# The gated one-hot of a PEER router: one VectorE instruction per token in place of a compare and a ScalarE product

## The chip, the cores and the metric

The kernel runs on one core of a Trainium2 chip. The metric is the device time of one execution in microseconds, given as the median of several runs. Engines are named as in the profile: PE is TensorE (PEld its weight loads), DVE is VectorE, ACT is ScalarE, POOL is GpSimd, and SP issues DMAs.

## What is computed

Two layers, each a mixer with four branches followed by a PEER product-key expert layer, on 512 positions of width 1024. The change lies in the PEER part:

```
sc = einsum("thpd,pkd->thpk", q, sub_keys)            # 8 heads, 2 x 128 keys
s_top, i_top = top_k(sc, 16)
best, pos = top_k(all 16 x 16 sums of s_top, 16)
idx  = i_top0[pos // 16] * 128 + i_top1[pos % 16]      # expert number: first key * 128 + second key
gate = softmax(best)
act  = gelu(expert_u[idx] . h) * gate
out  = sum over the chosen experts of act * expert_v[idx]
```

There are 16384 experts, and each position chooses 128 of them (8 heads with 16 each), every choice with its gate.

## The kernel before

For the first three tiles of 128 positions (ND = 3) the experts are computed densely: `up` multiplies every block of 128 experts with the 384 positions, and the result is later multiplied by a gate matrix that is zero for experts that were not chosen. The fourth tile is computed by gathering expert rows (`gathered`), one row of each position at a time.

All bulk matrix products go through `Stream`: `load` brings 512 KB of weights by an SP DMA, `split` makes two parts of them, `wh` by an ACT cast (L108) and `wl` by a DVE subtraction (L109), and the PE does three products (L120, L122, L123). One call of `bulk` is called a **bulk** below: in the stretch in question it has 24 matmuls of 384 columns, eight on L120 and eight each on L122 and L123. `advance` splits the weights two bulks ahead (SA = 2); there are three `wh` buffers and two `wl` buffers. After a bulk, `up` evicts the result by an ACT activation (L1278) and stores it.

Work that isn't bulk runs beside it: generators are put into `Beside`, and before every bulk `tick` takes as many of their pieces as a rate allows. So the order of instructions on each engine is fixed in the program: pieces of the generators, the bulk's matmuls, the split for two bulks later, the eviction. Each engine takes its instructions strictly in that order.

`Router.dense` builds the gate matrix at rate RG = 3.1. For each of the three tiles it first runs `pairs` (candidates, top 16, softmax: a long run of DVE instructions), then transposes the first key, the second key and the gate into `RT`, and then does 32 **steps** of four positions each. A step compares a row of numbers 0..127 (`iota`) with the keys of each position, which gives for each position two one-hot matrices of 128 choices by 128 keys (`oh`, DVE, L1229). The one of the first key is multiplied by the gates (ACT, L1232, four instructions, each in place). Five steps later (LAG = 5) the PE multiplies the two for each of the four positions (L1218), and ACT copies the sum into the gate matrix `GB` (L1220). A step costs 1.3 of the rate, so two or three steps fall to one bulk. At the end of a tile the last five steps have no one-hot of their own and come together. Six such runs of 32 steps exist, three in each layer. Beside them runs `gathered` at rate 0.8: a POOL gather (L1250) and a DVE product with a sum (L1259) for one row.

Of the kernel before, what the change touches and what calls it, by code (L numbers as in the profile page):

```python
# [13 lines left out]
AF = mybir.ActivationFunctionType  # L14
OP = mybir.AluOpType
# [51 lines left out]
def bc(ap, shape):  # L67
    return ap.to_broadcast(shape)
# [256 lines left out]
def small(e, name, shape):  # L325
    return e.ps.tile(list(shape), F32, name=name, tag="s")
# [770 lines left out]
class Router:  # L1097
# [89 lines left out]
    def dense(self, gbp, GB0):  # L1187

        e, pb, l = self.e, self.pb, self.l
        nc = e.nc  # L1190
        V = nc.vector
        stores = []
        iota = pb.tile([128, 128], F32, name="iota128", bufs=1)
        nc.gpsimd.iota(iota, pattern=[[1, 128]], base=0, channel_multiplier=0, allow_small_or_imprecise_dtypes=True)

        def store(i, n):
            if i % n == 1 and stores:
                stores.pop(0)()
        for t in range(ND):
            R = pb.tile([128, 4, 128], F32, name="R")  # L1200
            for i, cost in enumerate(self.pairs(t, R)):
                store(i, 4)
                yield cost
            yield 3.5
            pt = small(e, "rT", [128, 3, 128])
            for i in range(3):
                nc.tensor.transpose(pt[:, i], R[:, i], e.ident)
            RT = pb.tile([128, 3, 128], F32, name="RT", bufs=1)
            nc.scalar.copy(RT, pt)
            yield  # L1210
            GB = gbp.tile([128, 2, 128, 64], F32, name="GB", tag="GB")
            ohs = {}
            for q in range(32 + LAG):
                if q >= LAG:
                    pg = small(e, "G", [128, 4, 128])
                    oh = ohs.pop(q - LAG)
                    for a in range(4):
                        nc.tensor.matmul(pg[:, a], oh[:, 1, a], oh[:, 0, a], start=True, stop=True)  # L1218
                    h, o = divmod((q - LAG) * 4, 64)
                    nc.scalar.copy(GB[:, h, :, o:o + 4], pg.rearrange("p a i -> p i a"))  # L1220
                    if o == 60 and t < ND - 1:
                        for i in range(0, 128, 32):
                            stores.append(lambda i=i, t=t, h=h, GB=GB: nc.scalar.dma_start(
                                e.dG[l][t, h][:, i:i + 32], GB[:, h, i:i + 32]))
                store(q, 3)
                if q < 32:

                    oh = ohs[q] = pb.tile([128, 2, 4, 128], F32, name="oh", tag="oh", bufs=OH)
                    V.tensor_tensor(out=oh, in0=bc(iota[:, None, None, :], [128, 2, 4, 128]),  # L1229
                                    in1=bc(RT[:, 0:2, q * 4:q * 4 + 4, None], [128, 2, 4, 128]), op=OP.is_equal)  # L1230
                    for a in range(4):
                        nc.scalar.activation(oh[:, 0, a], oh[:, 0, a], AF.Copy, scale=RT[:, 2, q * 4 + a:q * 4 + a + 1])  # L1232
                yield 1.3 if q < 32 else 0.2
        for f in stores:
            f()
        e.GB = GB
# [128 lines left out]
def peer(e, l, src, dst, out):  # L1365
# [4 lines left out]
    with ExitStack() as st:  # L1370
# [5 lines left out]
        with pool("rt") as p1, pool("rtb", 2) as pb, pool("ga", 2) as ga:  # L1376
            SC = gbp.tile([128, 16, NT, 128], F32, name="SC", tag="GB")
            r = Router(e, l, p1, pb, SC)
            sc = r.scores()
            for hp in range(16):  # L1380
                r.query(hp)
                if hp == 0:
                    B.add(sc, 1.0, 1)
            b = 0
            for b in range(2):
                up(e, l, b, ga)
            B.finish(sc)
            R = pb.tile([128, 4, 128], F32, name="R")
            first = B.add(r.pairs(NT - 1, R), RF)
            for b in range(2, 2 + NB1):  # L1390
                up(e, l, b, ga)
            B.finish(first)
            if l:
                V.tensor_scalar(R[:, 3], R[:, 3], float(l * 16384), None, op0=OP.add)
            V.tensor_copy(e.gidx, R[:, 3])
            V.tensor_copy(e.ggate, R[:, 2])
            dense = B.add(r.dense(gbp, None), RG)
            rows = B.add(gathered(e, l), RU)
            for b in range(2 + NB1, NS):
                up(e, l, b, ga)  # L1400
            B.finish(dense)
# [177 lines left out]
```

## Time and profile before

| what | us |
|---|---|
| median of 3 runs | 4107.23 |
| lowest and highest run | 4102.68 and 4108.01 |
| the profiled execution | 4096.73 |
| its span, first to last instruction | 4095.0 |
| PE busy | 3905.9 (95%) |
| DVE busy | 3105.0 (76%) |
| ACT busy | 1688.7 (41%) |
| POOL busy | 1625.0 (40%) |
| L1229, the compare, 192 times | 225.0 (1219 ns each) |
| L1232, the product, 768 times | 244.4 (392 ns each) |

Busy time is the time in which an engine has an instruction of its own running; records of the PE overlap, so a busy PE isn't a PE at its peak. The chain that ended last names the PE for most of what it could follow, so a stage is read by asking what the PE does there and what it waits for. The mean granted clock of the PE was 0.982 of full speed.

### The profile page before, as it was taken

How to read it: one execution, taken by the hardware profiler on the slowest of the kernel's cores; microseconds unless marked ns; L12 is line 12 of the kernel's file. 1: busy time of each engine (PE TensorE's matmuls, PEld its weight loads, DVE VectorE, ACT ScalarE, POOL GpSimd, SP SyncE). 2: the span in 40 equal slices, each digit the busy share in tenths (PEclk: the TensorE clock that was granted, in tenths of full speed). 3: DMA queues.
4: the chain of work that ended last, by engine and by line, in shares of the span. 5: the costliest groups of instructions: out<-in, count | busy, mean ns of one | idle time of the engine just before them, and what ended most of it. 6: DMA issues, size and time to landing. Idle time of an engine off the chain costs nothing. (4 is left out here: it accounts for less than half of the span.)

```text
span 4095.0 us, 56429 instructions
## 1 busy us (share of the span) xinstructions
PE 3905.9 (95%) x19994; PEld 3384.6 (83%) x19994; DVE 3105.0 (76%) x5101; ACT 1688.7 (41%) x2939; POOL 1625.0 (40%) x1566
## 2 busy tenths in 40 slices
PE   7899999999999999999989999999999999999998
PEld 5777777899998899888767777878999898998876
DVE  5667844898878677889867777448978877788997
ACT  4323233336575533333343233333365664333333
POOL 3410500022313467888653014000323225678995
PEclk9999999999999999999999999999999999999999
DMA  3323333346876799999923233342568768999997
GB/s 112 102 81 101 101 96 109 115 162 204 293 235 221 254 325 319 351 356 339 325 69 105 91 95 101 98 134 85 182 213 274 249 207 285 323 321 349 335 340 262
DMA packets 346651, 851.40 MB, mean 208 GB/s; under 512 B 43648, under 2 KB 164864, under 8 KB 342016
## 3 DMA queue, kind: packets, MB, share of 16 engines
q1 hardware_dynamic: 236048, 492.39, 36.1%
q0 software_dynamic: 74016, 272.66, 19.5%
q10 hardware_dynamic: 36304, 82.74, 5.5%
q8 instruction: 158, 2.59, 0.3%
q14 instruction: 125, 1.02, 0.1%
HBM read 754.60 MB, written 93.06 MB: 207 GB/s over the span
## 5 line engine op out<-in xcount | busy, mean ns | idle before, releaser
L109 DVE TENSOR_TENSOR wl<-wr,wh 128x1024 fp32r<-128x1024 f32 (+2 forms) x792 | 987.3, 1247 | 528.7 <-ACT wh L108 453.8
L122 PE MATMUL mm<-hh,wh 128*128 128x384 f32 (+1 forms) x3456 | 1240.8, 359 | 0.0
L123 PE MATMUL mm<-hl,wh 128*128 128x384 f32 (+1 forms) x3456 | 1239.9, 359 | 0.0
L108 ACT CAST wh<-wr 128x1024 fp32r<-128x1024 f32 (+2 forms) x792 | 787.8, 996 | 338.9 <-PE va L132 127.8
L120 PE MATMUL mm<-hh,wl 128*128 128x384 f32 (+1 forms) x3456 | 792.2, 371 | 68.6 <-DVE wl L109 64.0
L120 PEld LDWEIGHTS mm<-hh,wl 128*128 128x128 f32 x3456 | 623.1, 191 | 150.7 <-DVE wl L109 81.3
L122 PEld LDWEIGHTS mm<-hh,wh 128*128 128x128 f32 x3456 | 655.8, 190 | 56.9
L123 PEld LDWEIGHTS mm<-hl,wh 128*128 128x128 f32 x3456 | 654.9, 190 | 56.1
L1250 POOL DMA_INDIRECT row<-in_u_dram,gidx x256 | 345.3, 1349 | 721.9 <-DVE row L1259 664.0
L132 PE MATMUL va<-wh,al 128*128 128x512 f32 x1536 | 598.1, 389 | 1.3 <-DVE al L109 1.3
L131 PE MATMUL va<-wh,ah 128*128 128x512 f32 x1536 | 597.9, 389 | 0.0
L1169 POOL TENSOR_TENSOR eq<-eq,cidx 128x800 f32<-128x800 f32 x64 | 126.2, 1977 | 891.4 <-DVE eq L1167 885.7
L1250 POOL DMA_INDIRECT row<-in_v_dram,gidx x256 | 383.2, 1497 | 103.8 <-DVE gacc L1270 47.0
L1270 DVE SCALAR_TENSOR_TENSOR gacc<-row,z,gacc 128x1024 f32<-128x1024 f32 x254 | 394.6, 1553 | 11.8 <-DMA row<-in_v_dram,gidx 10.1
L129 PE MATMUL va<-wl,ah 128*128 128x512 f32 x1536 | 395.0, 391 | 4.8 <-DVE wl L109 3.3
L1259 DVE SCALAR_TENSOR_TENSOR row<-row,h2row 128x1024 f32<-128x1024 f32 x256 | 339.3, 1335 | 1.2 <-DMA row<-in_u_dram,gidx 1.1
L132 PEld LDWEIGHTS va<-wh,al 128*128 128x128 f32 x1536 | 288.3, 188 | 62.7 <-DVE al L109 1.7
L129 PEld LDWEIGHTS va<-wl,ah 128*128 128x128 f32 x1536 | 285.4, 188 | 66.1 <-issue 11.0
L131 PEld LDWEIGHTS va<-wh,ah 128*128 128x128 f32 x1536 | 288.3, 188 | 60.7
L108 ACT CAST ah<-as 128x384 fp32r<-128x384 f32 x256 | 130.9, 511 | 480.7 <-POOL as L1321 266.9
L109 DVE TENSOR_TENSOR al<-as,ah 128x384 fp32r<-128x384 f32 x256 | 172.5, 674 | 193.6 <-ACT ah L108 185.5
L1232 ACT ACTIVATE oh<-oh,RT 128x128 f32<-128x128 f32 x768 | 244.4, 392 | 100.4 <-DVE oh L1229 100.4
(345 smaller groups left out, 4472.6 us busy)
## 6 DMA issues: line engine op xcount, KB each, us to landing
wr<-in_uT_dram SPq DMA_DIRECT2D x256, 512.0 KB
wr<-in_v_dram SPq DMA_DIRECT2D x256, 512.0 KB
wr<-in_w_in_dram SPq DMA_DIRECT2D x144, 512.0 KB
dS<-act ACTq DMA_DIRECT2D x184, 192.0 KB
as<-dS SPq DMA_DIRECT2D x184, 192.0 KB
dG<-GB ACTq DMA_DIRECT2D x32, 1024.0 KB
ag<-dG SPq DMA_DIRECT2D x128, 256.0 KB
wr<-in_w_query_dram SPq DMA_DIRECT2D x32, 512.0 KB
```

The costliest lines, as they stand in the source:

```text
L108: e.nc.scalar.copy(hi, src)
L109: e.nc.vector.tensor_tensor(out=lo, in0=src, in1=hi, op=OP.subtract)
L120: e.nc.tensor.matmul(ps, al, bh, start=start and i == 0, stop=False)
L122: e.nc.tensor.matmul(ps, ah, bh, start=False, stop=False)
L123: e.nc.tensor.matmul(ps, ah, bl, start=False, stop=stop and i == n - 1)
L129: e.nc.tensor.matmul(ps, ah, bl, start=start, stop=False)
L131: e.nc.tensor.matmul(ps, ah, bh, start=False, stop=False)
L132: e.nc.tensor.matmul(ps, al, bh, start=False, stop=stop)
L1232: nc.scalar.activation(oh[:, 0, a], oh[:, 0, a], AF.Copy, scale=RT[:, 2, q * 4 + a:q * 4 + a + 1])
L1250: nc.gpsimd.indirect_dma_start(out=g, out_offset=None, in_=e.I["u" if n < 128 else "v"], in_offset=bass.IndirectOffsetOnAxis(ap=e.gidx[:, ...
L1259: V.scalar_tensor_tensor(g, g, 1.0, e.h2row, op0=OP.mult, op1=OP.mult, accum_out=z[:, k:k + 1])
L1270: V.scalar_tensor_tensor(e.gacc, g, z[:, k:k + 1], e.gacc, op0=OP.mult, op1=OP.add)
```

## The change

The compare on L1229 now makes only the one-hot of the second key (512 elements per partition where there were 1024). The one-hot of the first key and its product with the gate become one DVE instruction for each position: `iota` is compared with the key and the result is multiplied by the gate, and both are read as one value per partition from `RT`. The four ACT instructions of a step are gone. Nothing else differs; lines below L1232 move down by one.

```
                     oh = ohs[q] = pb.tile([128, 2, 4, 128], F32, name="oh", tag="oh", bufs=OH)
-                    V.tensor_tensor(out=oh, in0=bc(iota[:, None, None, :], [128, 2, 4, 128]),
-                                    in1=bc(RT[:, 0:2, q * 4:q * 4 + 4, None], [128, 2, 4, 128]), op=OP.is_equal)
+                    V.tensor_tensor(out=oh[:, 1], in0=bc(iota[:, None, :], [128, 4, 128]),
+                                    in1=bc(RT[:, 1, q * 4:q * 4 + 4, None], [128, 4, 128]), op=OP.is_equal)
                     for a in range(4):
-                        nc.scalar.activation(oh[:, 0, a], oh[:, 0, a], AF.Copy, scale=RT[:, 2, q * 4 + a:q * 4 + a + 1])
+                        t_ = slice(q * 4 + a, q * 4 + a + 1)
+                        V.tensor_scalar(oh[:, 0, a], iota, RT[:, 0, t_], RT[:, 2, t_], op0=OP.is_equal, op1=OP.mult)
```

On DVE, near the start of the first 32 steps, this stood between two splits of weights (`wl` is the split, `row` the gathered row's product) before the change:

```order
L109 TENSOR_TENSOR wl<-wr,wh 128x1024
L1229 TENSOR_TENSOR oh<-iota_7354,RT 128x1024 x3
L1259 SCALAR_TENSOR_TENSOR row,z<-row,h2row 128x1024
L109 TENSOR_TENSOR wl<-wr,wh 128x1024
L1229 TENSOR_TENSOR oh<-iota_7354,RT 128x1024 x2
```

and this stands there now:

```order
L109 TENSOR_TENSOR wl<-wr,wh 128x1024
L1229 TENSOR_TENSOR oh<-iota_7354,RT 128x512
L1233 TENSOR_SCALAR oh<-iota_7354,RT 128x128 x4
L1229 TENSOR_TENSOR oh<-iota_7354,RT 128x512
L1233 TENSOR_SCALAR oh<-iota_7354,RT 128x128 x4
L1229 TENSOR_TENSOR oh<-iota_7354,RT 128x512
L1233 TENSOR_SCALAR oh<-iota_7354,RT 128x128 x4
L1260 SCALAR_TENSOR_TENSOR row,z<-row,h2row 128x1024
L109 TENSOR_TENSOR wl<-wr,wh 128x1024
```

Five instructions stand where one stood, at the same place between the splits. On ACT, in the same bulks, between the casts `wh` of two bulks (`act` is the eviction of a bulk, `dS` its store), there stood before:

```order
L108 CAST wh<-wr 128x1024
L1278 ACTIVATE act<-mm 128x384
L1279 DMA dS_27_254<-act 128x384
L1220 COPY GB<-G 128x128x4
L1232 ACTIVATE oh<-oh,RT 128x128 x4
L1220 COPY GB<-G 128x128x4
L1232 ACTIVATE oh<-oh,RT 128x128 x4
L1220 COPY GB<-G 128x128x4
L1232 ACTIVATE oh<-oh,RT 128x128 x4
L108 CAST wh<-wr 128x1024
```

and now:

```order
L108 CAST wh<-wr 128x1024
L1279 ACTIVATE act<-mm 128x384
L1280 DMA dS_27_254<-act 128x384
L1220 COPY GB<-G 128x128x4 x3
L108 CAST wh<-wr 128x1024
```

Between two casts ACT has no instruction left that waits for DVE's one-hots.

## Rows read from the trace of the kernel before

**Rows 1.** Windows: us; busy us (count) of PE, PEld, DVE, ACT, POOL; clock; DMA
```profile
962.30:1051.75 89.45, 86.24 (x569) 85.29 (x568) 62.11 (x65) 69.21 (x179) 10.07 (x11) 0.98 0.67 215
...
1273.60:1362.90 89.30, 82.48 (x546) 81.13 (x545) 63.11 (x67) 69.67 (x179) 11.09 (x12) 0.96 0.56 172
...
sum 537.90, PE 507.81 PEld 500.63 DVE 376.20 ACT 417.87 POOL 62.92; mean PE 84.63 PEld 83.44 DVE 62.70 ACT 69.64 POOL 10.49
```

**Rows 2.** Windows of line 120 alone, the same stretches: eight matmuls make one bulk
```profile
962.30:1051.75 89.45, 22.09 (x104) 18.03 (x104) 0.98 0.67 215
...
1273.60:1362.90 89.30, 19.82 (x96) 16.28 (x97) 0.96 0.56 172
```

**Rows 3.** Timeline of PE: start, us, engine, line, operation; two places
```profile
1131.02 1.30 PE L120 MATMUL mm<-hh,wl 128*128 128x384 f32 x6
...
1135.30 2.84 PE L1218 MATMUL G<-oh 128*128 128x128 f32 x24
1137.89 1.66 PE L120 MATMUL mm<-hh,wl 128*128 128x384 f32 x8
...
1372.85 1.55 PE L120 MATMUL mm<-hh,wl 128*128 128x384 f32 x8
...
1377.01 1.20 PE L120 MATMUL mm<-hh,wl 128*128 128x384 f32 x6
```

**Rows 4.** Waits, 940 to 1420 us: who waited for whom, us, times, longest
```profile
DVE wl L109 <- ACT wh L108: 93.4, 47, 4.1
...
PE mm L120 <- DVE wl L109: 21.9, 18, 3.4
...
PE G L1218 <- ACT oh L1232: 7.8, 7, 2.6
```

**Rows 5.** Timeline of ACT from one cast of weights to the next
```profile
1336.77 1.03 ACT L108 CAST wh<-wr 128x1024 fp32r<-128x1024 f32 x1
...
1340.23 1.28 ACT L1232 ACTIVATE oh<-oh,RT 128x128 f32<-128x128 f32 x4 [1.06 <-DVE oh L1229]
1341.42 0.56 ACT L1220 COPY GB<-G 128x512 f32<-128x512 f32 x1
1341.88 1.28 ACT L1232 ACTIVATE oh<-oh,RT 128x128 f32<-128x128 f32 x4
1343.07 1.03 ACT L108 CAST wh<-wr 128x1024 fp32r<-128x1024 f32 x1
```

**Rows 6.** Timeline of DVE in the same bulk
```profile
1337.83 1.23 DVE L109 TENSOR_TENSOR wl<-wr,wh 128x1024 fp32r<-128x1024 f32 x1 [3.31 <-ACT wh L108]
1338.97 2.35 DVE L1229 TENSOR_TENSOR oh<-iota,RT 128x1024 f32<-128x1024 f32 x2
1341.24 1.22 DVE L1259 SCALAR_TENSOR_TENSOR row<-row,h2row 128x1024 f32<-128x1024 f32 x1
```

**Rows 7.** Timeline of DVE at three places with short TENSOR_SCALAR instructions
```profile
1.25 0.22 DVE L79 TENSOR_SCALAR tri<-ji 128x128 f32<-128x128 int32 x1
1.39 0.22 DVE L81 TENSOR_SCALAR strict<-ji 128x128 f32<-128x128 int32 x1
...
275.71 0.88 DVE L916 TENSOR_SCALAR yd<-cfx,par 128x512 f32<-128x512 f32 x2
276.50 0.75 DVE L920 SCALAR_TENSOR_TENSOR yd<-cfx,par,yd 128x512 f32<-128x512 f32 x1
...
385.45 0.43 DVE L216 TENSOR_SCALAR rsv<-rsa 128x512 int32<-128x512 int32 x1
385.92 0.43 DVE L217 TENSOR_SCALAR rsv<-rsv 128x512 int32<-128x512 int32 x1
386.26 1.22 DVE L109 TENSOR_TENSOR wl<-wr,wh 128x1024 fp32r<-128x1024 f32 x1
```

**Rows 8.** Timeline of all engines around one gather on POOL
```profile
1262.29 1.68 POOL L1250 DMA_INDIRECT row<-in_u_dram,gidx  x1 [2.24 <-DVE row L1259]
...
1263.42 0.21 DVE L1177 TENSOR_SCALAR R<-R 128x128 f32<-128x128 f32 x1
...
1263.66 0.35 DVE L1178 TENSOR_SCALAR R<-R 128x128 f32<-128x128 f32 x1
```

## The prediction, made before the run

> **What bounds the kernel now.** I read first the slices of the page, where the steps of `dense` can be found as the two places in which ACT is busiest, then the busy time of each engine in the six runs of 32 steps, each cut from the start of the first bulk ahead of it to the start of the first bulk behind it. Together the six last 537.9 us, and in them DVE is busy for 376.2 and ACT for 417.9 [rows 1]. No engine is full there by its own row except, seemingly, PE (507.8); but records of PE overlap, so I ask what PE needs at the least.
>
> A bulk without steps starts 4.16 us after the one before it; one with three steps in front of it (24 records of L1218) starts 6.87 us after [rows 3]. So a step costs PE (6.87 - 4.16) / 3 = 0.90. L120 counts 104 records, 13 bulks, in four of the runs and 96, 12 bulks, in two [rows 2]: 76 bulks and 6 x 32 = 192 steps. **PE needs 76 x 4.16 + 192 x 0.90 = 316.2 + 172.8 = 489.0 us. It takes 537.9, so 48.9 are lost.** Part of this is the clock: it was granted at 0.96 to 0.98 in the two runs shown [rows 1], that is at the lower of its two levels for a few per cent of the time, behind pauses of PE.
>
> What PE waits for are `wl` from DVE and the one-hots from ACT, and far more time than either DVE waits for ACT's cast `wh`: 93.4 us in layer 0, about 2 us a time [rows 4]. The timelines of ACT and DVE in one bulk show why [rows 5, 6]. The cast starts at 1336.77; `wl` needs it and starts at 1337.83; behind `wl` in DVE's order comes the one-hot, at 1338.97; ACT stands idle until its product can begin, at 1340.23; then a copy (1341.42), the next product (1341.88), and only then the next cast, at 1343.07. This is a ring through two engines: each waits for the other once in a bulk, and neither is full. It takes 6.30 us with two steps, and a third adds copy and product, 0.46 + 1.19 = 1.65. With 192 / 76 = 2.53 steps in a bulk that is 6.30 + 0.53 x 1.65 = 7.17, where PE needs 4.16 + 2.53 x 0.90 = 6.44. The 0.73 x 76 = 56 us is close to the 48.9 lost; the difference is the lead with which DVE enters a run, since weights are split two bulks ahead. So the steps are bound by the ring, not by an engine.
>
> **The change, part by part.** *ACT loses* four products in each step. They lie 1.19 us in ACT's order [rows 5], 192 x 1.19 = 228 us in all. As work this is worth nothing, since ACT isn't full; what it opens is the ring. Of ACT's work between two casts (a copy for each step, an eviction, a store) nothing waits for DVE any more. The cast of two bulks ahead can start when PE has done the steps in front of the bulk, while the split made from it is needed two bulks later. PE's products now wait for DVE directly.
>
> *DVE loses* half of L1229. Two of them take 1341.24 - 1338.97 = 2.27, so 1.135 each [rows 6]. Short instructions that don't depend on each other start 0.14 apart at 128 elements and 0.34 at 512 (L79 to L81, and L217 to L109) [rows 7], so the part that doesn't grow with size is 0.07; the half compare is then (1.135 - 0.07) / 2 + 0.07 = 0.60.
>
> *DVE gains* four instructions of 128 elements in each step. Call the distance of their starts d. With constants it would be 0.14. A value read per partition costs more: L916 reads one, and two of them take 276.50 - 275.71 = 0.79, 0.395 each, against 0.34 with constants [rows 7]: 0.055 for one. The new form reads two; no row shows that. From below d is 0.195, if both are read at once. From above, if each instruction had to wait for the one before it to end, as L217 does for L216 (0.47 against 0.34, 0.13 more [rows 7]), it is 0.14 + 0.13 + 0.11 = 0.38. I take 0.25, two reads at their own price, because the four don't depend on each other, as the independent rows don't.
>
> DVE's work in the six runs is then 376.2 - 192 x 1.135 + 192 x (0.60 + 4 d) = 158.3 + 192 x (0.60 + 4 d):
> at d = 0.195 it is 423, at 0.25 it is 466, at 0.38 it is 565. It reaches PE's 489.0 at d = 0.28 and today's 537.9 at d = 0.344. At my value DVE is 95% full but below PE, so PE becomes the bound. The added 90 us of DVE work are hidden by the 162 us in which DVE now stands idle in these runs; with that cover gone they would land on the path.
>
> *The ends of the runs.* The last five or six steps come together, and PE needs the last one-hots while they are new. Before, they came through ACT: 7.8 us of waits in layer 0 [rows 4]. Now they come from DVE one engine earlier, but behind more DVE work. I leave 1 us for each of the six ends.
>
> *Between the runs* (`pairs`) nothing is changed. DVE enters with the lead that the run's end leaves, so I count nothing there; it could give or take a few us.
>
> *POOL.* The short DVE form may stand in POOL's way. In the rows one of them ran inside a gather in 0.21, while another, at the gather's end, took 0.35, 0.14 more [rows 8]. With at most 12 gathers in a run by POOL's count [rows 1], 72 x 0.14 = 10 us: 466 becomes 476, still under 489.
>
> The Trainium skill, "SBUF — State Buffer", section "Who interferes with whom", speaks against this change: VectorE's `tensor_scalar` on two SBUF ports and a GpSimd instruction lock each other out for the whole instruction. The row agrees only at the gather's end; the 0.21 inside it does not fit a lock from start to end.
>
> **Sum.** 48.9 lost, less 6 at the ends, about 42 us gained. The profiled execution took 4096.73 us (span 4095.0), so it would take 4055; the median of the runs lies 10.5 us above it, and taking the gain from there gives 4107 - 42 = **4065**. A difference of 0.2%, 8 us, is about what a measurement of this kernel can tell from no change.
>
> **Rivals.** *Part of the gain only.* For: the new form, with a compare and two values per partition, may not run at the rate of the plain ones. From 128 to 512 elements they took 0.20 more, so 128 elements cost 0.067, and at half that rate d is 0.25 + 0.067 = 0.317: DVE needs 158.3 + 192 x 1.868 = 517, 21 us are gained, 4086. Against: L916 with its value per partition shows no slower rate.
>
> *POOL holds DVE back.* If a gather stopped the short DVE instructions for all of its time, POOL's 62.9 us in these runs [rows 1] would be added: 466 + 63 = 529, 9 us gained, 4098. For: the 0.35 row; against: the 0.21 row. (This is the skill's lock, above; by d = 0.195 the sum would be 486 and nothing would be lost.)
>
> *Slower.* The four instructions run one behind the other's end instead of overlapping, d = 0.38 by the dependent rows: DVE becomes the bound of the steps at 565, 27 us above today, 4134. It decides from d = 0.344 on. For: DVE has little to spare, and five instructions replace one. Against: the order shows no wait between them, and the independent rows overlap.
>
> *No change.* d near 0.34, or DVE meets its lead used up in the runs of `pairs` and gives back there what it gained: 4107.
>
> **How the numbers follow.** Forecast, PE-bound steps, 4052 to 4078: 0.68. Part of the gain, 4079 to 4098: 0.10 by a slower rate and 0.05 by POOL. Within 0.2%: 0.08. Slower: 0.09. Faster by over 0.2% is 0.83, the same 0.08, slower 0.09. The range runs from 4050, all 48.9 us and some 8 more from a better lead into `pairs`, to 4104, which takes in the partial cases and leaves out the slow one.
>
> **What would show it.** Right: the six runs shrink from 89 to about 82 us each, with DVE busy over 90% of them; L1233 starts every 0.20 to 0.25 us; DVE's wait for `wh` falls from 93 us in layer 0 to under 20; PE's waits for `wl` inside the runs go, while those in `pairs` stay; the clock in the runs is near 1.00. Wrong: L1233 at 0.3 us or more apart, with PE still waiting for `wl` in the runs and DVE without idle time; or runs that shrink while the stretches between them grow.

## The result, and the profile after

The changed kernel takes **4040.07 us** (median of 4 runs, 4033.05 to 4047.63) where the kernel before takes 4104.95 in the same comparison. The ratio is 0.985 with a 95% interval of 0.983 to 0.987: 65 us faster. The forecast was 4065, with a range from 4050, so the sign was right and the gain was half again as large as forecast, 10 us beyond the low end of the range. A later comparison gave 4037.15 for the same kernel.

The profiled execution took 4033.05 us. The top of its page, against the table of before: ACT fell from 1688.7 to 1477.9, DVE rose from 3105.0 to 3217.4, and the span is 63.7 us shorter.

```profile
span 4031.3 us, 56403 instructions
...
PE 3877.6 (96%) x19994; PEld 3363.8 (83%) x19994; DVE 3217.4 (80%) x5869; ACT 1477.9 (37%) x2171; POOL 1697.8 (42%) x1566
```

The six runs of 32 steps, cut as in [rows 1] from bulk start to bulk start; two of them and the sum (us; busy us and count of PE, PEld, DVE, ACT, POOL; granted clock; DMA share and GB/s):

```profile
962.67:1045.57 82.90, 82.90 (x569) 82.90 (x569) 81.33 (x209) 37.48 (x59) 17.74 (x12) 1.00 0.71 247
...
1253.80:1332.52 78.72, 78.72 (x546) 78.72 (x545) 76.62 (x187) 36.03 (x56) 19.44 (x12) 1.00 0.57 195
...
sum 489.04, PE 489.04 PEld 489.04 DVE 477.46 ACT 221.59 POOL 111.09; mean PE 81.51 PEld 81.51 DVE 79.58 ACT 36.93 POOL 18.52
```

The six now last 489.0 us together, to the decimal what the prediction said that PE needs, where they lasted 537.9. A run of 13 bulks takes 13 x 4.16 + 32 x 0.90 = 82.9, and one of 12 takes 78.7: PE waits for nothing any more, the clock is at 1.00 of its upper level, and DVE, 98% busy, is just fast enough.

The end of the first run on PE shows the same rates as [rows 3], now without exception: 6.86 from 1030.95 to the next bulk with three steps in front of it, 7.76 with four.

```profile
1030.95 1.66 PE L120 MATMUL mm<-hh,wl 128*128 128x384 f32 x8
...
1035.22 2.84 PE L1218 MATMUL G<-oh 128*128 128x128 f32 x24
1037.81 1.66 PE L120 MATMUL mm<-hh,wl 128*128 128x384 f32 x8
...
1042.09 3.73 PE L1218 MATMUL G<-oh 128*128 128x128 f32 x32
1045.57 1.66 PE L120 MATMUL mm<-hh,wl 128*128 128x384 f32 x8
```

The waits of layer 0 (us, times, longest), from 940 to 1390: `wl` waits for the cast 18.4 us where it waited 93.4 in [rows 4], and PE's wait for one-hots has no row left. PE's wait for `wl`, 9.9 us where it was 21.9, is now zero inside the runs.

```profile
DVE wl L109 <- ACT wh L108: 18.4, 10, 3.9
...
PE mm L120 <- DVE wl L109: 9.9, 10, 3.3
```

One bulk on DVE, which answers to [rows 6]. From 1318.72 to 1319.74 four short instructions take 1.02, the compare of the other half from 1318.12 takes 0.60, and nothing in the row is idle:

```profile
1318.12 0.68 DVE L1229 TENSOR_TENSOR oh<-iota,RT 128x512 f32<-128x512 f32 x1
1318.72 1.11 DVE L1233 TENSOR_SCALAR oh<-iota,RT 128x128 f32<-128x128 f32 x4
1319.74 1.22 DVE L1260 SCALAR_TENSOR_TENSOR row<-row,h2row 128x1024 f32<-128x1024 f32 x1
...
1320.89 1.22 DVE L109 TENSOR_TENSOR wl<-wr,wh 128x1024 fp32r<-128x1024 f32 x1
```

**Where the time came from.** Layer 0 in pieces, all from starts of L120 on PE's timeline; layer 1 repeats it. The *tail* is the last bulk interval of a run, with the last 4, 5 and 6 steps in it.

| piece of layer 0 | before | after | gained |
|---|---|---|---|
| run 1 without its tail, tail | 79.52, 9.90 | 75.14, 7.76 | 4.38, 2.14 |
| run 2 | 78.39, 11.70 | 74.25, 8.65 | 4.14, 3.05 |
| run 3 | 71.74, 17.53 | 69.17, 9.55 | 2.57, 7.98 |
| `pairs` between runs 1 and 2 | 62.32 | 58.98 | 3.34 |
| `pairs` between runs 2 and 3 | 69.47 | 66.35 | 3.12 |
| three bulks behind run 3 | 14.07 | 12.59 | 1.48 |
| sum | | | 32.2 |

Twice 32.2 is 64.4, against 63.7 measured between the two spans. Of that 22 us come from inside the runs, 26 from the tails, 13 from `pairs` and 3 from behind the third run. The last two, 16 us, stand in no term of my sum. The pieces are far steadier than the total: in a second trace of the changed kernel, of 4044.73 us, all of them repeat to 0.1 us, while the stretch from the end of the last run to the end of the kernel, with nothing changed in it, takes 706.6 us where it takes 697.4 in this one.

Before, the third tail cost most. PE waited there twice for products on ACT:

```profile
1354.93 3.72 PE L1218 MATMUL G<-oh 128*128 128x128 f32 x16 [2.39 <-ACT oh L1232]
...
1361.22 2.07 PE L1218 MATMUL G<-oh 128*128 128x128 f32 x8 [2.57 <-ACT oh L1232]
```

and the clock came down with these pauses: the eight matmuls of L120 right behind this tail, at 1362.94, take 2.91, and those right ahead of it, at 1345.41, took 1.68. The windows of this tail and of the three bulks behind it (columns as above) have 0.80 and 0.89 of the clock, where both have 1.00 now:

```profile
1345.41:1362.94 17.53, 12.52 (x72) 11.74 (x73) 12.64 (x14) 13.56 (x37) 2.67 (x3) 0.80 0.63 196
1362.94:1377.01 14.07, 14.07 (x74) 14.07 (x74) 7.11 (x9) 5.54 (x10) 4.31 (x6) 0.89 0.76 219
```

**Why `pairs` gained, though nothing in it was changed.** In the kernel before DVE is 98% busy there, 60.93 of 62.32 us. So it bounds that stretch, and what DVE has done ahead of time at its entry is worth its length. The first row is of before, the second, in a fence of its own, of after; DVE has 4.6 us less left to do:

```profile
1051.79:1114.11 62.32, 56.51 (x318) 54.32 (x317) 60.93 (x143) 26.04 (x39) 33.26 (x19) 1.00 0.86 294
```

```profile
1045.57:1104.55 58.98, 56.19 (x319) 54.31 (x317) 56.37 (x125) 23.22 (x30) 32.27 (x18) 1.00 0.85 291
```

How far DVE is ahead shows in one pair of rows each: the split `wl`, and the bulk that uses it, the second behind the first run. Before, the split ended at 1052.94 + 1.22 = 1054.16 for a bulk at 1056.04, a **lead** of 1.88:

```profile
1052.94 1.22 DVE L109 TENSOR_TENSOR wl<-wr,wh 128x1024 fp32r<-128x1024 f32 x1 [2.13 <-ACT wh L108]
...
1056.04 1.55 PE L120 MATMUL mm<-hh,wl 128*128 128x384 f32 x8
```

After, it ended at 1041.78 for a bulk at 1049.84, a lead of 8.06:

```profile
1040.56 1.22 DVE L109 TENSOR_TENSOR wl<-wr,wh 128x1024 fp32r<-128x1024 f32 x1
...
1049.84 1.55 PE L120 MATMUL mm<-hh,wl 128*128 128x384 f32 x8
```

Six us more lead brought three us: in the new trace DVE's next split, at 1047.97, has waited 2.72 for a cast that ACT starts only at 1046.89, behind its copies of the tail's last sums (the last at 1045.85). So there is a limit to what a lead can hand on.

### The profile page after: what moved, and what is told of

Same layout as the page of the kernel before. It is cut to its first block, busy times and chain, and to the rows that moved or that the text cites. A ratio compares the mean times of both kernels' runs of the same rounds, so it can differ in the third digit from the quotient of the medians.

```text
span 4031.3 us, 56403 instructions
## 1 busy us (share of the span) xinstructions
PE 3877.6 (96%) x19994; PEld 3363.8 (83%) x19994; DVE 3217.4 (80%) x5869; ACT 1477.9 (37%) x2171; POOL 1697.8 (42%) x1566
## 3 DMA queue, kind: packets, MB, share of 16 engines
q14 instruction: 124, 1.02, 0.1%
## 4 chain that ended last, share of the span: by engine, by line
PE 74%; DVE 13%; POOL 5%; issue 4%; DMA 3%; ACT 2%; SPq 0%; DVEq 0%; POOLq 0%; ACTq 0%
PE mm L120 14%; PE mm L123 13%; PE mm L122 13%; PE va L129 6%; PE va L132 6%; PE va L131 6%; PE G L1218 4%; DVE wl L109 3%; PE pb L120 2%; DMA as<-dS 1%; PE pb L123 1%; PE pb L122 1%; DVE row L1260 1%; DMA row<-in_v_dram,gidx 1%; POOL as L1322 1%
## 5 line engine op out<-in xcount | busy, mean ns | idle before, releaser
L120 PE MATMUL mm<-hh,wl 128*128 128x384 f32 (+1 forms) x3456 | 787.0, 370 | 46.2 <-DVE wl L109 42.4
L120 PEld LDWEIGHTS mm<-hh,wl 128*128 128x128 f32 x3456 | 619.8, 190 | 123.4 <-DVE wl L109 54.1
L1251 POOL DMA_INDIRECT row<-in_u_dram,gidx x256 | 389.4, 1521 | 611.1 <-DVE row L1260 561.7
L1251 POOL DMA_INDIRECT row<-in_v_dram,gidx x256 | 397.4, 1552 | 97.9 <-DVE gacc L1271 44.8
L1271 DVE SCALAR_TENSOR_TENSOR gacc<-row,z,gacc 128x1024 f32<-128x1024 f32 x254 | 413.3, 1627 | 20.4 <-DMA row<-in_v_dram,gidx 18.8
L1322 POOL TENSOR_TENSOR as<-as,GB 128x128 f32<-128x128 f32 x256 | 263.8, 1030 | 0.0
```

Of the source, the lines that this page charges most:

```text
L120: e.nc.tensor.matmul(ps, al, bh, start=start and i == 0, stop=False)
L1251: nc.gpsimd.indirect_dma_start(out=g, out_offset=None, in_=e.I["u" if n < 128 else "v"], in_offset=bass.IndirectOffsetOnAxis(ap=e.gidx[:, ...
L1271: V.scalar_tensor_tensor(e.gacc, g, z[:, k:k + 1], e.gacc, op0=OP.mult, op1=OP.add)
L1322: G.tensor_tensor(out=s[:, 4:6], in0=s[:, 4:6], in1=self.e.GB[:, :, (i + NS) % 128], op=OP.mult)
```

## The experiments

The theory: the runs were bound by a ring, ACT's cast, DVE's split and one-hot, ACT's product, the next cast; cut it, and PE is the bound. DVE's rate decides whether it stays so, and DVE's lead is a store that runs hand on to `pairs`. The rivals: ACT's 228 us of work were what counted, not where they stood; DVE's new instructions have a cost of their own; a gain goes by the number of changed steps, whatever their place.

The kernels that test the theory, in one table: length of the three runs of layer 0 (tail in brackets) and of the two stretches of `pairs`, in us.

| kernel | run 1 | run 2 | run 3 | `pairs` | median |
|---|---|---|---|---|---|
| before | 89.42 (9.90) | 90.09 (11.70) | 89.27 (17.53) | 62.32, 69.47 | 4096 to 4105 |
| after | 82.90 (7.76) | 82.90 (8.65) | 78.72 (9.55) | 58.98, 66.35 | 4040.07 |
| product one step later | 82.90 (7.76) | 82.90 (8.65) | 78.72 (9.55) | 58.95, 66.35 | 4033.53 |
| product three steps later | 87.25 (9.05) | 89.11 (10.69) | 83.75 (12.38) | 58.93, 66.34 | 4067.73 |
| ring put back | 84.08 (8.93) | 84.81 (10.20) | 81.83 (12.66) | 62.26, 69.43 | 4059.72 |
| one DVE instruction more | 86.08 (9.65) | 86.75 (10.70) | 85.90 (16.16) | 61.18, 67.79 | 4072.54 |
| two more | 94.05 (9.78) | 94.70 (10.65) | 93.50 (18.95) | 61.43, 68.06 | 4126.99 |
| late half | 84.21 (7.76) | 84.10 (8.65) | 79.88 (10.71) | 60.58, 67.77 | 4050.96 |
| early half | 83.71 (8.57) | 84.67 (10.42) | 84.22 (15.05) | 62.32, 69.41 | 4070.62 |

### The ring, or ACT's work?

**The kernel before, with ACT's product one step later.** All of ACT's work stays, DVE's too; the product of a step is only written behind the next step's compare, so ACT finds its one-hot ready.

```
+                if 1 <= q < 33:
+                    o2, p = ohs[q - 1], q - 1
                     for a in range(4):
-                        nc.scalar.activation(oh[:, 0, a], oh[:, 0, a], AF.Copy, scale=RT[:, 2, q * 4 + a:q * 4 + a + 1])
+                        nc.scalar.activation(o2[:, 0, a], o2[:, 0, a], AF.Copy, scale=RT[:, 2, p * 4 + a:p * 4 + a + 1])
```

> As the run with ACT's product three steps later, but one step later. There, with three steps in a bulk, the third G on PE waited for a product that ACT made only behind the copy of the first G, 0.57 us a bulk. With one step later the product is due four steps ahead of its G, and ACT's product still needs only one-hots that DVE made a step earlier. Theory (rings, not ACT's amount of work): no ring is left, ACT's 6.0 us a bulk lie under PE's 6.44, the runs of steps take about 489 to 495 us and the kernel about 4040 to 4050 us, like the changed one with all of ACT's work kept. Rival (ACT's amount of work costs in itself): it stays at about 4068 as with three steps later, or above.

4033.53 us (4032.21 to 4037.09), ratio to before 0.984 [0.982, 0.986]. Its windows of runs 1 and 3 (columns as above) have the lengths of the changed kernel, with ACT as busy as ever (72.4 of 82.9 us) and DVE at 65.2 instead of 81.3:

```profile
965.20:1048.10 82.90, 82.90 (x569) 82.90 (x569) 65.24 (x83) 72.38 (x184) 12.14 (x11) 1.00 0.75 247
1256.30:1335.02 78.72, 78.72 (x546) 78.72 (x545) 62.07 (x65) 69.19 (x179) 11.87 (x12) 1.00 0.61 197
```

So ACT's 228 us were worth nothing as work. The place of the wait was all, and no work had to be moved to another engine.

**The same, three steps later.** The edit is the one above with 3 for 1.

> The kernel before, all its work kept; only ACT's product of a step is written three steps later, so ACT no longer waits in the same bulk for the one-hot that DVE makes behind the split. Theory (a ring through ACT and DVE bound the steps): ACT's own work is 0.93 + 0.5 + 0.4 + 2.53 x 1.65 = 6.0 us a bulk, under PE's 6.44, so the six runs of steps shrink from 538 to about 489 us, DVE enters the stretches of pairs with its full lead, and the kernel takes about 4040 us like the changed one (up to 4055 if the ends of the runs wait for ACT). Rival (it was the amount of ACT's work that had to go): ACT still does 418 us in the runs, and the time stays at about 4105.

4067.73 us (4062.91 to 4071.81), ratio 0.992 [0.990, 0.994]: about half the gain, and above the 4055 that was allowed. `pairs` has all of it, the runs have not: a bulk with three steps takes 7.44 instead of 6.87. ACT and PE in one such bulk:

```profile
993.39 3.41 PE L1218 MATMUL G<-oh 128*128 128x128 f32 x24
...
994.50 0.58 ACT L1220 COPY GB<-G 128x512 f32<-128x512 f32 x1 [0.42 <-PE G L1218]
994.98 1.28 ACT L1234 ACTIVATE oh<-oh,RT 128x128 f32<-128x128 f32 x4
995.43 1.17 PEld L1218 LDWEIGHTS G<-oh 128*128 128x128 f32 x8 [0.29 <-ACT oh L1234]
```

The product at 994.98 stands on ACT behind the copy of the bulk's first sum, at 994.50, and PE needs it for the third sum of the same bulk (995.43). I had cut one ring and closed another, between PE and ACT. A wait that is moved must not land on work that another engine needs in the same bulk.

**The changed kernel with the ring put back.** Behind the four DVE instructions ACT copies each result onto itself.

```
                         V.tensor_scalar(oh[:, 0, a], iota, RT[:, 0, t_], RT[:, 2, t_], op0=OP.is_equal, op1=OP.mult)
+                    for a in range(4):
+                        nc.scalar.activation(oh[:, 0, a], oh[:, 0, a], AF.Copy, scale=1.0)
```

> The changed kernel with four ACT instructions a step put back, a copy of the finished one-hot in place by a factor 1.0. Theory: the ring is closed again, with a longer DVE leg (compare and four short instructions, 1.63 us, for 1.135): 6.30 + 0.49 = 6.79 us with two steps, 7.66 on the mean, 76 bulks 582 us for 545; the kernel takes about 4120 to 4145 us, slower than before. Rival (amount of ACT's work): about 4105, as before. Rival (the gain came from DVE's new form): about 4040.

4059.72 us (4057.39 to 4068.99): 20 lost, not 80 to 105. The expectation fell, not by the mechanism but by the size of the ring, which ACT's timeline gives:

```profile
1021.13 1.04 ACT L108 CAST wh<-wr 128x1024 fp32r<-128x1024 f32 x1
...
1024.32 1.08 ACT L1235 ACTIVATE oh<-oh 128x128 f32<-128x128 f32 x4 [0.78 <-DVE oh L1233]
1025.31 0.57 ACT L1220 COPY GB<-G 128x512 f32<-128x512 f32 x1
1025.95 1.08 ACT L1235 ACTIVATE oh<-oh 128x128 f32<-128x128 f32 x4
1026.94 1.04 ACT L108 CAST wh<-wr 128x1024 fp32r<-128x1024 f32 x1
```

Cast to cast is 5.81 us with two steps (and 7.44 with three, to 1034.38), less than the 6.30 and 7.95 of before: ACT's first copy waits only for the first of the four short instructions, and with a constant factor the four take 0.99 of ACT's order, where they took 1.19. The mean is 5.81 + 0.53 x 1.63 = 6.67 against PE's 6.44, 0.23 a bulk and 3 us a run. DVE enters a run 2 to 4 us ahead (leads read as above, at the first bulk of each run), and so the body of run 1 loses nothing (84.08 - 8.93 = 75.15, against 75.14). What is lost is lost when the lead is gone: 5.8 us in the three tails and 6.4 in the two stretches of `pairs` of layer 0, 24 in both layers. This was the first sign that a ring slower than PE is paid behind the run.

### How near is DVE to being the bound?

**One and two of the four short instructions written twice.** `for a in [0, 1, 2, 3, 0]` and `for a in [0, 1, 2, 3, 0, 1]` in place of `range(4)`.

> The changed kernel with one of the four short DVE instructions of each step done twice. Theory: DVE becomes the bound of the steps where its sum passes PE's 489 us: 158.3 + 192 x (0.60 + 5 x 0.257) = 520 us, 31 more than PE needs, and DVE enters pairs without a lead, 16 more: about 4085 (4070 to 4095). Rival (DVE has slack of its own once the ring is open): 4040 to 4050.

> The changed kernel with two of the four short DVE instructions of each step done twice. Theory: DVE's sum is 158.3 + 192 x (0.60 + 6 x 0.257) = 570 us, 81 more than PE needs, with the lost lead about 4136 us (4120 to 4145), slower than the kernel before. Rival (slack of its own): under 4080.

4072.54 us (4067.35 to 4081.04; ratio 0.993 [0.991, 0.995]) and 4126.99 (4126.34 to 4128.90; ratio 1.007 [1.005, 1.008], slower than before). By the prediction's formula with d = 0.257 as now measured, DVE needs 158.3 + 192 x (0.60 + 5 x 0.257) = 520 us and 570 in the six runs; they took 516 and 564, both kernels within the times expected. The third run with two more (columns as above) has DVE 93.05 busy of 93.50:

```profile
1282.26:1375.76 93.50, 83.82 (x546) 81.85 (x545) 93.05 (x249) 36.02 (x56) 18.65 (x12) 0.95 0.48 165
```

Five short instructions cost what four at d = 0.32 would, six what four at 0.386 would: this is the *slower* rival, which the prediction priced at 4134 for d = 0.38. It was the right rival; the reserve in front of it is 4% of DVE.

**Fewer values read per partition.** In the first kernel the gate is a constant, in the second the key and the gate are, so the first leaves out the gates and the second the first keys too.

```
-  V.tensor_scalar(oh[:, 0, a], iota, RT[:, 0, t_], RT[:, 2, t_], op0=OP.is_equal, op1=OP.mult)
+  V.tensor_scalar(oh[:, 0, a], iota, RT[:, 0, t_], 1.0, op0=OP.is_equal, op1=OP.mult)
...
+  V.tensor_scalar(oh[:, 0, a], iota, 5.0, 1.0, op0=OP.is_equal, op1=OP.mult)
```

> The changed kernel with the gate left out of the one-hot (the second value of the short DVE instruction is the constant 1.0), for the price of one value read per partition; the output lacks the gates. Each at its own price: the starts lie 0.195 us apart, for 0.257 with two. Both read at once: 0.257 or close to it. The time of the kernel stays at about 4040, since PE bounds the steps either way.

> The changed kernel with both values of the short DVE instruction constants (5.0 and 1.0); the keys and gates of the first one-hot are left out. The starts lie 0.14 us apart by the short instructions of the trace; the time of the kernel stays at about 4040 (4030 to 4045), since DVE is no bound.

Four instructions together, one row each from DVE's timeline: 0.87 us with one value,

```profile
1317.01 0.87 DVE L1233 TENSOR_SCALAR oh<-iota,RT 128x128 f32<-128x128 f32 x4
```

and 0.63 with none, against 1.11 with two in the row at 1318.72 above:

```profile
1318.36 0.63 DVE L1233 TENSOR_SCALAR oh<-iota 128x128 f32<-128x128 f32 x4
```

Less the length of the last (0.22, 0.28 and 0.34, the medians), over three distances, d is (0.63 - 0.22) / 3 = 0.137, (0.87 - 0.28) / 3 = 0.197 and (1.11 - 0.34) / 3 = 0.257: **0.060 for each value**. A second operation costs nothing that shows: with one operation, L79 to L81 in [rows 7], the distance is 0.14 as well. The times are 4031.65 and 4037.14, one execution each, within the spread of the changed kernel, and the six runs last 489.0 us in both: DVE's relief is worth nothing while PE is the bound.

### Where the further gain came from

**The new form for half of each run.** The late half has it for steps 16 to 31 and the old form before (the diff); the early half has `q < 16` in the condition.

```
+                    if q >= 16:
                         V.tensor_tensor(out=oh[:, 1], in0=bc(iota[:, None, :], [128, 4, 128]),
...
+                    else:
+                        V.tensor_tensor(out=oh, in0=bc(iota[:, None, None, :], [128, 2, 4, 128]),
+                                        in1=bc(RT[:, 0:2, q * 4:q * 4 + 4, None], [128, 2, 4, 128]), op=OP.is_equal)
+                        for a in range(4):
+                            nc.scalar.activation(oh[:, 0, a], oh[:, 0, a], AF.Copy, scale=RT[:, 2, q * 4 + a:q * 4 + a + 1])
```

> Edit: steps 0 to 15 of each run keep the old one-hot with its product on ACT, steps 16 to 31 take the new DVE form. My theory (DVE's lead over PE is a store: it is used up in the first half of a run of before, only then does PE lose time, and the lead at the run's end is what shrinks the stretch of pairs behind it): in the kernel before, the lead fell from 3.6 us to 0.05 in about half a run and PE had lost next to nothing by then, so the first half costs 1 to 2 us a run, 6 to 12 in all; the second half rebuilds some 0.4 us a bulk and has no waits in its tail; about 3 to 6 us of lead at the entry to pairs keep about half of the 12.8 us gained there. 4040 + 9 + 6 = 4055 (4048 to 4062). Rival (each changed step is worth the same, wherever it stands): half of the 65 us gained, 4072, the same as the early half.

> Edit: steps 0 to 15 of each run take the new DVE form, steps 16 to 31 the old one-hot with its product on ACT. My theory: the first half loses nothing and leaves a lead of about 6 us; the second half uses it up at 0.2 to 0.7 us a bulk, and the tail of 4 to 6 steps waits for the ring as in the kernel before, 2 to 3 us a run, 15 in all; the lead at the entry to the first pairs is back at 2 to 3 us, so most of the 12.8 us there are lost. 4040 + 15 + 12 = 4067 (4060 to 4075), over 8 us slower than the late half. Rival (each changed step is worth the same): 4072, the same as the late half.

Beside the changed kernel at 4037.15 and the one before at 4098.15, the late half took **4050.96** us (4042.95 to 4054.21) and the early half **4070.62** (4069.28 to 4074.57). The rival, equal shares, said 4072 for both; they lie 20 us apart, and in the order of the store. The late half loses 1.3, 1.2 and 0 us inside its runs and 1.2 in its tails, and keeps half of the gain in `pairs`. The early half loses nothing inside its runs, then 8 us in the three tails of layer 0, all of `pairs`, and 2 us behind the third run. Run 1 and `pairs` of the late half (columns as above),

```profile
962.02:1046.23 84.21, 83.44 (x570) 83.06 (x569) 70.00 (x130) 54.20 (x120) 11.83 (x11) 1.00 0.69 230
1046.23:1106.81 60.58, 56.17 (x318) 54.30 (x317) 60.34 (x143) 23.14 (x32) 34.49 (x19) 1.00 0.86 296
```

and of the early half:

```profile
962.22:1045.93 83.71, 83.43 (x570) 83.23 (x569) 69.31 (x123) 51.93 (x118) 14.54 (x11) 1.00 0.66 227
1045.93:1108.25 62.32, 57.63 (x318) 55.75 (x318) 60.92 (x147) 26.18 (x36) 33.21 (x19) 0.97 0.86 291
```

The stretch of `pairs` is the same code in both, and differs by 1.7 us with the steps that run just ahead of it. The lead at the second bulk, read as above, tells the lengths apart in all kernels at once:

| kernel | split starts, takes | bulk starts | lead | first `pairs` |
|---|---|---|---|---|
| early half | 1047.09, 1.23 | 1050.18 | 1.86 | 62.32 |
| before | 1052.94, 1.22 | 1056.04 | 1.88 | 62.32 |
| ring put back | 1047.52, 1.22 | 1050.63 | 1.89 | 62.26 |
| two more | 1058.33, 1.24 | 1062.32 | 2.75 | 61.43 |
| one DVE instruction more | 1050.92, 1.24 | 1055.18 | 3.02 | 61.18 |
| late half | 1045.64, 1.22 | 1050.50 | 3.64 | 60.58 |
| product one step later | 1044.87, 1.23 | 1052.37 | 6.27 | 58.95 |
| after | 1040.56, 1.22 | 1049.84 | 8.06 | 58.98 |
| product three steps later | 1046.96, 1.22 | 1056.27 | 8.09 | 58.93 |

Up to 3.64 a us of lead is a us of `pairs`; from 6.27 on more lead brings nothing. Kernels with ACT's products stand at both ends of the table, so it is the lead that counts here and not which engine makes the product.

### Can it be faster?

**Thinner `pairs`, denser steps.** Where `pairs` is bound by DVE and the runs by PE, work may be shifted between them by the costs that the planner counts: a piece of `pairs` 1.4 to 1.6 (CP), a step 1.3 to 1.15, and the rate of the `pairs` that come first 3.2 to 3.6 (RF). First in the changed kernel, then in the kernel before with its product one step later.

```
-RU, RB, RV, RG, RF = 0.8, 1.42, 1.1, 3.1, 3.2
+RU, RB, RV, RG, RF = 0.8, 1.42, 1.1, 3.1, 3.6
...
-CP = 1.4
+CP = 1.6
...
-                yield 1.3 if q < 32 else 0.2
+                yield 1.15 if q < 32 else 0.2
```

> The changed kernel with the pieces of pairs spread over more bulks (their cost 1.4 to 1.6 of the rate, RF 3.2 to 3.6 so that the first pairs end where they did) and the steps put closer (1.3 to 1.15). In pairs DVE is the bound, and what is left there is about 4.7 + 7.9 us a layer; in the runs PE then has 2.7 steps a bulk, 6.59 us, and DVE 6.52. Theory: about 10 to 15 us of the waits in pairs go, 4025 to 4035 us. Rival (DVE, 99% full, falls behind in the runs and meets pairs without a lead): 4040 to 4060.

> Edit: the kernel before with its ACT product written one step later (which alone gave 4033.53), and the planner's numbers for the steps that spread the last ones over more bulks (which took the changed kernel from 4040 to 4028.2). Theory: the steps are bound by PE with either form, so the spread is worth the same here, 5 to 12 us: 4021 to 4029. Rival: the products on ACT in the tail are needed while they are new, and with the tail spread ACT's four copies stand in the way of more casts and evictions, so the spread is worth nothing here: 4032 to 4038.

> No edit: the changed kernel again, beside the other three. 4033 to 4047 by the runs so far; the comparison with the two halves and with the spread version is made against this one.

On the changed kernel: **4028.20** us (4026.57 to 4029.64), ratio 0.983 [0.980, 0.985], 9 to 12 us under the two medians of the changed kernel (4040.07 and 4037.15), with intervals that overlap. The runs now have 12, 11 and 11 bulks instead of 13, 13 and 12, and from the start of run 1 to three bulks behind run 3 PE loses 9.6 us a layer instead of 13.2 (374.7 us for 67 bulks and 96 steps, which need 365.1, against 382.4 for 68 bulks, which need 369.3). That is 7 us in both layers, most of the 9 to 12. Run 1 and the `pairs` behind it:

```profile
963.83:1042.54 78.71, 78.71 (x545) 78.71 (x545) 77.46 (x207) 35.99 (x57) 14.39 (x9) 1.00 0.66 235
1042.54:1108.23 65.69, 64.01 (x366) 62.70 (x365) 63.26 (x137) 25.38 (x33) 33.33 (x19) 1.00 0.87 303
```

On the kernel before with its product one step later it is open: 4032.94 us in the median, against 4033.53 without the new costs, but the profiled execution took 4018.52 and the other three 4032.83 to 4033.64. The trace, of the 4018.52 alone, has 8.7 us lost a layer, where 13.1 were lost without; what the other three executions did differently no trace shows. Part of the 4018.52 may be chance: the stretch behind the last run took 690.7 us there and 702.5 in the trace without the new costs, and it differs by 9 us between the two traces of the changed kernel.

## Why the prediction was right, and where it was not

*The bound, and the 48.9 us.* Right to the decimal: the six runs shrank from 537.9 to 489.0, and the gain in them is 48.9. That the place of the wait mattered and not ACT's work was right as well (4033.53 with all of ACT's work kept).

*The ring's own size.* Right in kind, but the agreement of 56 with 48.9 was in part chance. The ring works inside a run, where 22 us were lost; 26 us were lost in the tails, by waits for ACT's products and by the clock that came down with them. I read the tails as a small thing to come (below), and took all of the loss as the ring's rate.

*DVE's price.* d was taken as 0.25 and is 0.257; the half compare as 0.60 and is 0.60; two values at 0.055 each, and each costs 0.060. DVE's need comes to 471 us instead of 466, still under 489. Neither of the bounds 0.195 and 0.38 came; the second would have made the kernel slower, as six short instructions showed.

*POOL.* I put 10 us of DVE at risk; DVE paid nothing that shows (the longest L1233 is 356 ns, the median 342). It was POOL that took longer, see below, under cover of its own idle time.

*The ends of the runs: the term that was mis-sized.* "I leave 1 us for each of the six ends", six in all; they cost 0. The tails of 7.76, 8.65 and 9.55 are 4.16 + 4, 5 and 6 x 0.90, with no wait. DVE has the last one-hots done early, because it is 6 to 8 us ahead when the tails begin (leads read as above).

*Between the runs: the step that failed.* "DVE enters with the lead that the run's end leaves, so I count nothing there; it could give or take a few us." It gave 12.9 us. I named the mechanism and didn't follow it: the run's end would leave far more lead, and `pairs` was at 98% of DVE in the trace of before. Both were to be had: one more window over the stretch behind each run shows 60.93 of 62.32, and the 5% of reserve that I gave DVE is 4 us of lead over a run's 83 us.

*Behind the third run* 3 us came that I had no term for: before, PE ran there at 0.89 of its clock after the pauses of the tail.

48.9 + 12.9 + 3 = 64.8 is the gain; I had 48.9 - 6. The **low end**, "all 48.9 us and some 8 more", held too little for `pairs` and for what lies behind the third run, 16 us where I allowed 8. The *rivals* (part of the gain, POOL, slower, no change) did not come; all were on the other side of the forecast, and none asked what would be better than expected. Of the signs I had listed, the clock, the runs' lengths, DVE's share and its waits came as said; L1233 starts every 0.257, just above the 0.20 to 0.25. One did not come, and it belongs to the step that failed: PE's waits for `wl` in `pairs` were to stay, and they fell from 5.3 and 6.0 us in the two stretches of layer 0 to 2.3 and 3.7.

## What to carry to other kernels

Where two engines wait for each other once in a round, ask which wait closes the ring before moving work: writing one product a step later did all that the new instruction did, with DVE's reserve kept. And a stretch that gets faster on an engine hands its lead on, so read the busy share of that engine in the stretch behind it too: at 98% each us of lead was worth a us here, up to a limit, and a stage that loses nothing itself may still pay later.

## What the hardware showed besides

- A DVE instruction of 128x128 costs 0.060 us more for each value that it reads per partition (d of 0.137, 0.197, 0.257). On ACT a factor per partition costs 82 ns of an instruction's length, 392 for the product (L1232, before) and 310 for the same with a constant, but only 0.05 us back to back, where four took 1.19 and 0.99. The Trainium skill, "ScalarE: Activation LUTs", section "What ACT_TABLE_LOAD costs", puts about 93 ns on each such operand; the 82 ns here are near it.
- The gather on POOL became longer, 1349 to 1521 ns, in the pages of before and after (first row before, second after; count, busy us, mean ns, idle before it):

```profile
L1250 POOL DMA_INDIRECT row<-in_u_dram,gidx x256 | 345.3, 1349 | 721.9 <-DVE row L1259 664.0
```

```profile
L1251 POOL DMA_INDIRECT row<-in_u_dram,gidx x256 | 389.4, 1521 | 611.1 <-DVE row L1260 561.7
```

All 68 gathers that start in the six runs of before take 0.94 us, while DVE stands idle. Of the 72 of after, 62 take 1.68, each started some 0.35 us into a split, and the ten that start while DVE is idle take 0.94. One of before, and one of after, to which the split at 1320.89 above belongs:

```profile
1342.74 0.94 POOL L1250 DMA_INDIRECT row<-in_u_dram,gidx  x1 [13.31 <-DVE row L1259]
```

```profile
1321.24 1.68 POOL L1251 DMA_INDIRECT row<-in_u_dram,gidx  x1 [5.49 <-DVE row L1260]
```

DVE's split takes 1.22 either way. This fits the Trainium skill, "SBUF — State Buffer", section "Who interferes with whom", by which a DVE instruction with two SBUF inputs contends with a GpSimd instruction that reads SBUF, and the order of issue decides who is blocked: here DVE, whose split has two SBUF inputs, is first, and POOL pays. I had cited the section as a danger for DVE. Which part of a gather waits is not shown.
